# A hybrid encoder layer on one core: taps from on-chip tiles, bias halves, spreads by transposes, value products moved ahead

## The chip, the cores and the metric

The kernel runs on one core of one Trainium2 chip. The core has TensorE (PE, matrix products; its weight loads are listed apart as PEld), VectorE (DVE), ScalarE (ACT), GpSimd (POOL) and SyncE (SP, which only issues transfers here). Data lives in DRAM, in the on-chip memory of 128 partitions, and in eight banks in which TensorE leaves its sums. POOL and SP issue the transfers, each from a queue in program order. The metric is the time of one execution in microseconds on the device. Before the change the median of three runs is 2327.94 us (2321.54 to 2329.34).

## The reference

One layer of an encoder over 2048 frames of width 1024. After one RMS norm a single projection feeds two groups:

```python
h = rmsnorm(x, norm_mix_g)
proj = h @ w_in                     # u_ssm (512) | q (512) | k (512) | v (512)
y_ssm = s5_mixer(u_ssm, ...)        # 32 groups of 16 channels, 64 complex states each
y_att = chunked_attention(q, k, v, rel_bias)   # 8 heads of 64
x = x + concat(rmsnorm(y_ssm), rmsnorm(y_att)) @ w_out
h2 = rmsnorm(x, norm_ffn_g)
x = x + (silu(h2 @ w_gate) * (h2 @ w_up)) @ w_down
return rmsnorm(x, norm_final_g)
```

The state space group computes `b_bar = (exp(lam dt) - 1) / lam * b`, runs the recurrence `state = lam_bar * state + b_bar u`, and puts out `Re(C state) + D u`, then a GELU and a sigmoid gate. In attention each chunk of 64 frames sees itself and the 8 chunks before it, and every score gets a bias of its head, indexed by the distance clipped to 128:

```python
rel = arange(576)[None, :] - 512 - arange(64)[:, None]
bias = rel_bias[:, clip(rel, -128, 128) + 128]
scores = q @ k.T / 8 + bias ;  probs = softmax(scores)
```

## The kernel before

All products are float32 made of three passes over operands split into a rounded high part and a low part (`split`, `mm3`): high by high, high by low, low by high. TensorE's products go through `Ordered`, so their order is the order in which the program states them; the other engines' instructions are placed by a scheduler, with `high_priority` pulling some ahead.

`u_phase` computes the state space input. It walks four blocks of 512 frames in the order 1, 2, 3, 0. `prep(b)` loads eight tiles `xt` (a ring of four), scales and splits them, and loads the rows of `x` for the sums of squares. `group(b, f)` is one product of 128 outputs by 512 frames, 24 passes, and a block has four. `finish(b)` spreads the block's reciprocal roots over the partitions (`spread_`, which calls `spread`) and scales and stores the four results to `u`. Between the groups `long(n)` advances `n` steps of `ssm_prologue`.

`ssm_prologue` makes the constants of the state space part. Its elementwise work on VectorE gives powers `pr`, `pi` of `lam_bar` and the scaled input matrix `bbr`, `bbi`. Each tile holds two groups of a pair: partitions 0 to 63 one, 64 to 127 the other. `v` (four blocks `b_`, from `cmul`) is the output side, stored to DRAM as `vs`, and `wt` the input side. The 32 tap matrices `kt` (16 by 128 each) are products of `bb` and `v` per group. For these the kernel stores `bbr` and `bbi` to DRAM (`bbs`), reloads them and `vs` with the real and imaginary halves of one group under one another on 128 partitions (`bbg`, `vg`), and takes one product per group. `transposes` turns the `wt` tiles and stores them as `bsts`. POOL fills a table of powers `a8`. The last steps run inside the first query product, where `PRO` says how many follow each of its steps.

`att_phase` runs 128 steps (4 blocks by 8 heads by 4 query tiles). A step s takes the scores of its tile (`scores`), the transposes of step s - 2 (`transp`), the value products of a finished head (`pv_head`), once in two heads the division by the softmax sums (`pv_scale`), and then a share of the units: projections of queries, keys and values, and eight state space units (`ssm_unit`) of 15 steps, whose recurrence runs on POOL. A `Unit` counts how many of its steps are due at s; the first value projection `v0` has 17 and is due in steps 0 to 3. The scores bank is one buffer: VectorE adds the bias and takes the minimum out of it (line 829) before the next scores go in.

The bias of a head is a tile `nb` of 128 by 640. A preparation turns the table into rows `nbs` in DRAM (8 by 768), spreads them with a copy inside DRAM to `nbms`, row p shifted by p (line 521), and two more copies put 1e30 into two corners of each head (line 524), so that what lies outside the band drops out. `load_nb` (line 800) then loads one head's tile, two buffers in turn, two steps ahead.

A spread is four products of a column, repeated 128 times, with the identity: in `spread`, in `rstd_steps`, and in `pv_scale`.

After attention `mix_phase` gates, normalises and projects, and the gate, up and down products follow by a seven-product scheme; the change touches them only through the spreads.

Of the kernel before, what the change touches and what calls it, by code (L numbers as in the profile page):

```python
# [13 lines left out]
ALU = mybir.AluOpType  # L14
AX = mybir.AxisListType

P = 128
# [3 lines left out]
NG, CH, NS = 32, 16, 64  # L21
NPR = NG // 2
L = 8
# [24 lines left out]
V0 = 0, 4  # L48
DB, XB = 3, 2
# [15 lines left out]
LONG = 1, 3, 2  # L65
# [56 lines left out]
def spread(k, te, pb, o, c):  # L122

    for i in range(4):
        te.matmul(pb[:, i * P : (i + 1) * P], o[:, c + i : c + i + 1].to_broadcast([P, P]), k.ident[:], start=True, stop=True)


def rstd_steps(k, te, psum, pool, tag, sq, n, out, **kw):
# [11 lines left out]
    for i in range(nt):  # L140
        te.matmul(pb[:, i * P : (i + 1) * P], o[:, i : i + 1].to_broadcast([P, P]), k.ident[:], start=True, stop=True)
# [15 lines left out]
def ssm_prologue(k, ident, S):  # L157
# [3 lines left out]
    with tc.tile_pool(name="pro", bufs=1) as p:  # L161
# [126 lines left out]
        def transposes(b_, wt):  # L288
            bst = k.t(p, "v" if b_ > 1 else "vg", [P, 9 if b_ > 1 else 8, 2, NS], bufs=2)[:, :8]
# [42 lines left out]
        for g2 in range(2):  # L332
            for c, bt in ((0, bbr), (1, bbi)):
                nc.gpsimd.dma_start(S["bb"][:, g2, c].rearrange("q n m -> n q m"), bt[g2 * NS : (g2 + 1) * NS])
        yield
        wts = []
        for b_ in range(4):
            qs = slice(4 * b_, 4 * b_ + 4)
# [7 lines left out]
            yield  # L346
        for b_ in range(4):
            qs = slice(4 * b_, 4 * b_ + 4)
            wt = [k.t(p, f"wt{i}", [P, 4, L, CH], bufs=4) for i in range(2)]
            cmul(wt[0][:], wt[1][:], rc(pr, qs), rc(pi, qs), cc(bbr, qs, L), cc(bbi, qs, L), [4, L, CH])  # L350
            wts.append(wt)
            yield
# [13 lines left out]
        kt = k.t(p, "kt", [CH, 8, P], bufs=2)  # L366
        nc.gpsimd.memset(kt[:], 0.0)
        for b_ in range(4):
            nc.gpsimd.dma_start(S["kt"][:, 8 * b_ : 8 * b_ + 8, 0], kt[:])
        bb = k.t(p, "bbg", [P, NG, CH])  # L370
        nc.sync.dma_start(bb[:], S["bb"].rearrange("q g c n m -> (c n) (q g) m"))
        dm = k.t(p, "cm1", [P, 576])[:CH, : NG * CH].rearrange("c (g m) -> c g m", g=NG)
        V.tensor_tensor(dm, ident[:CH, :CH].unsqueeze(1).to_broadcast([CH, NG, CH]),
                        ddt[:].unsqueeze(2).to_broadcast([CH, NG, CH]), op=ALU.mult)
        vgs = []
        for b_ in range(4):
            vgs.append(k.t(p, "vg", [P, 8, P], bufs=2)[:] if b_ < 2 else k.t(p, "v", [P, 9, P], bufs=2)[:, :8])
            nc.sync.dma_start(vgs[b_], S["v"].rearrange("q g c n m -> (c n) (q g) m")[:, 8 * b_ : 8 * b_ + 8, :P])
        for b_ in range(4):
            gs = slice(8 * b_, 8 * b_ + 8)  # L380
            vg = vgs[b_]
            kt = k.t(p, "kt", [CH, 8, P], bufs=2) if b_ < 2 else k.t(p, ("bc", "small")[b_ - 2], [CH, 8, P])
            if b_ == 0:
                yield
            for g0 in (0, 4):
                ps = k.t(k.pro_psum, "pp", [P, 512])[:].rearrange("p (a b) -> p a b", a=4)
                for g in range(4):
                    k.te.matmul(ps[:CH, g, :], bb[:, 8 * b_ + g0 + g, :], vg[:, g0 + g, :], start=True, stop=True)
                nc.scalar.copy(kt[:, g0 : g0 + 4, :], ps[:CH])
                yield  # L390
            V.tensor_tensor(kt[:, :, :CH], kt[:, :, :CH], dm[:, gs], op=ALU.add)
            nc.gpsimd.dma_start(S["kt"][:, gs, 1], kt[:])
# [4 lines left out]
def u_phase(k, ident, S, aw):  # L397
# [3 lines left out]
    with ExitStack() as cx:  # L401
# [113 lines left out]
        for n in range(1, NSB):  # L515
            last, b = BLOCKS[n - 1 : n + 1]
            prep(b)
            if n == 1:
                corner = k.t(p1, "corner", [64, 64])
                nc.gpsimd.memset(corner[:], 1e30)  # L520
# [1156 lines left out]
```

## Time and profile before

| | us | where it is from |
|---|---|---|
| median of three runs | 2327.94 | times (2321.54 to 2329.34) |
| the profiled execution | 2328.99 | its own time |
| its span | 2327.2 | profile |
| TensorE busy | 2197.0 | page, part 1 |
| weight loads busy | 1852.3 | page, part 1 |
| VectorE busy | 1545.0 | page, part 1 |
| ScalarE busy | 1004.7 | page, part 1 |
| GpSimd busy | 349.0 | page, part 1 |
| mean granted clock of TensorE | 0.973 | cores view |

The busy time of an engine is the union of its instructions. Weight loads overlap products. A row of the stretch view gives, for a stretch of the span, the busy time of each engine with its count of instructions, the granted clock of TensorE (1.00 is full), the busy share of the 16 transfer engines, and GB/s. The chain of waits is followed back from the last instruction to what released it; a piece that begins with DMA is time in which the next engine waited for that transfer. A row of SP's queue shows the time taken to issue, not to land.

### The profile page before, as it was taken

What the parts mean: (1) busy time and instruction counts of PE and PEld (TensorE: products, weight loads), DVE (VectorE), ACT (ScalarE), POOL (GpSimd) and SP (SyncE); (2) the same over time, 40 slices, a digit from 0 to 9 for tenths busy, and PEclk for the clock granted to TensorE, in tenths of its full rate; (3) what the DMA queues carried; (4) which work ended last, traced back from release to release, by engine and by line L of the source; (5) the groups of instructions that cost most, each with busy time, mean ns of one, the idle gap of its engine ahead of it and who ended that gap; (6) DMA issues with size and microseconds to landing.
All of it is one profiled execution on the core that took longest, in us unless ns stands there. A gap on an engine that the chain in (4) does not pass through costs nothing.

```text
span 2327.2 us, 30433 instructions
## 1 busy us (share of the span) xinstructions
PE 2197.0 (94%) x10712; PEld 1852.3 (80%) x10712; DVE 1545.0 (66%) x2695; ACT 1004.7 (43%) x1655; POOL 349.0 (15%) x814
## 2 busy tenths in 40 slices
PE   8878899999997899999999999999999989999997
PEld 6766688898986688878888887888888878888886
DVE  7746545756545756777776668666756477789766
ACT  4435445555556752253333336333333343353321
POOL 3237545466542000000000000000000000000000
PEclk9989899999998999999999999999999999999998
DMA  8967676775654434763554647555423297465641
GB/s 274 291 221 249 194 209 196 200 221 176 193 153 146 141 105 149 245 198 127 182 180 149 235 160 284 183 198 163 167 90 114 68 338 255 163 216 186 227 158 73
DMA packets 225329, 434.90 MB, mean 187 GB/s; under 512 B 43480, under 2 KB 70152, under 8 KB 218072
## 3 DMA queue, kind: packets, MB, share of 16 engines
q1 hardware_dynamic: 220312, 418.79, 55.0%
q0 software_dynamic: 4864, 14.17, 1.9%
q8 instruction: 84, 1.38, 0.2%
q14 instruction: 69, 0.57, 0.1%
HBM read 292.88 MB, written 132.15 MB: 183 GB/s over the span
## 4 chain that ended last, share of the span: by engine, by line
PE 82%; DMA 6%; DVE 6%; POOL 2%; ACT 2%; issue 1%; SPq 1%; DVEq 0%; ACTq 0%; POOLq 0%
PE X L78 20%; PE ps L78 19%; PE Y L78 10%; PE pf L78 10%; PE big L78 9%; PE W L78 5%; PE pj L78 5%; PE sc L78 2%; PE pt L81 2%; DMA xt<-in_xp 2%; DMA xt<-in_xt 1%; DVE lo L154 1%; SPq L549 1%; DMA nb<-nbms 1%; DMA hd<-wc 0%
## 5 line engine op out<-in xcount | busy, mean ns | idle before, releaser
L78 PE MATMUL X<-hi,c 128*128 128x512 f32 x1408 | 451.3, 391 | 8.5 <-DVE c L154 6.9
L78 PE MATMUL ps<-hd,hd 128*128 128x512 f32 (+1 forms) x1968 | 432.0, 382 | 6.1 <-ACT hd L154 3.7
L78 PEld LDWEIGHTS ps<-hd,hd 128*128 128x128 f32 x1968 | 359.3, 190 | 77.5 <-ACT hd L154 4.6
L78 PEld LDWEIGHTS X<-hi,c 128*128 128x128 f32 x1408 | 265.6, 189 | 65.2 <-DVE c L154 7.8
L78 PE MATMUL X<-lo,c 128*128 128x512 f32 x704 | 274.9, 390 | 0.0
L154 ACT CAST hd<-hd 128x1536 fp32r<-128x1536 f32 (+1 forms) x106 | 147.6, 1393 | 238.1 <-DMA hd<-hq 181.9
L78 PE MATMUL Y<-hi,c 128*128 128x512 f32 x704 | 224.1, 389 | 1.5 <-DVE u L1367 1.5
L154 DVE TENSOR_TENSOR hd<-hd 128x1536 fp32r<-128x1536 f32 (+1 forms) x106 | 174.1, 1645 | 28.8 <-ACT hd L154 28.1
L154 DVE TENSOR_TENSOR c<-S,c 128x512 fp32r<-128x512 f32 x176 | 120.9, 688 | 104.1 <-ACT c L154 104.1
L829 DVE CUSTOM_DVE_ANT_0 s<-sc,nb 128x640 f32<-128x640 f32 (+4 forms) x128 | 94.5, 738 | 110.9 <-PE sc L78 98.7
L1491 DVE TENSOR_TENSOR acc<-acc,ps 128x512 f32<-128x512 f32 x196 | 131.3, 684 | 53.0 <-PE ps L78 48.3
L1363 ACT COPY u<-X 128x512 f32<-128x512 f32 x132 | 77.6, 588 | 204.9 <-PE X L78 204.8
L78 PE MATMUL big<-m,woh 128*128 128x512 f32 x512 | 162.7, 400 | 0.0
L78 PE MATMUL pf<-hi,w 128*128 128x512 f32 x416 | 153.1, 420 | 8.9 <-ACT w L154 4.6
L154 ACT CAST c<-S 128x512 fp32r<-128x512 f32 x176 | 109.5, 622 | 118.3 <-PE Y L78 67.0
L78 PEld LDWEIGHTS Y<-hi,c 128*128 128x128 f32 x704 | 132.1, 188 | 29.3 <-DVE u L1367 1.9
L78 PEld LDWEIGHTS X<-lo,c 128*128 128x128 f32 x704 | 132.8, 189 | 27.7
L154 ACT CAST c<-raw 128x512 fp32r<-128x512 f32 x132 | 82.2, 623 | 149.4 <-PE Y L78 71.2
L78 PE MATMUL Y<-lo,c 128*128 128x512 f32 x352 | 137.0, 389 | 0.0
L832 ACT ACTIVATE s<-s,mn 128x640 f32<-128x640 f32 (+4 forms) x128 | 98.0, 765 | 77.2 <-DVE mn L829 76.5
L848 DVE TENSOR_TENSOR ptl<-pt,pth 128x640 fp32r<-128x640 f32 (+3 forms) x152 | 98.3, 647 | 45.8 <-ACT pth L847 44.1
L847 ACT CAST pth<-pt 128x640 fp32r<-128x640 f32 (+3 forms) x152 | 83.7, 551 | 94.8 <-PE pt L81 89.5
(441 smaller groups left out, 4229.3 us busy)
## 6 DMA issues: line engine op xcount, KB each, us to landing
w<-wss SPq DMA_DIRECT2D x36, 1024.0 KB, 6.7
hq<-g SPq DMA_DIRECT2D x140, 256.0 KB, 2.2
hd<-hq SPq DMA_DIRECT2D x42, 768.0 KB, 4.4
hd<-wc SPq DMA_DIRECT2D x42, 768.0 KB, 6.0
raw<-in_w_gate SPq DMA_DIRECT2D x44, 512.0 KB, 3.7
raw<-in_w_up SPq DMA_DIRECT2D x44, 512.0 KB, 4.1
wc<-px SPq DMA_DIRECT2D x66, 256.0 KB, 3.2
wss<-w SPq DMA_DIRECT2D x12, 1024.0 KB, 6.0
```

The lines of the kernel that those rows point to most:

```text
L78: return self.tc.keep_in_program_order(self.tc.nc.tensor.matmul(*a, **b))
L81: return self.tc.keep_in_program_order(self.tc.nc.tensor.transpose(*a, **b))
L154: return nc.scalar.copy(hi, raw), nc.vector.tensor_tensor(lo, raw, f32(hi), op=ALU.subtract)
L549: ins = nc.sync.dma_start(out, in_)
L829: nc.vector.tensor_tensor_reduce(s[:, :nk].rearrange("p (a b) -> p a b", a=nch), ps[:, :nch, :half], hd.nb[:, nk - 1 :: -1].rearrange("p ( ...
L832: nc.scalar.activation(s[:, :nk], s[:, :nk], AF.Exp, bias=mn[:], scale=-1.0, accum_out=sums[sb, pr][:, hh, qp : qp + 1])
L847: nc.scalar.copy(pth[:, a:b, qp, :], pt[:, a:b, :])
L848: nc.vector.tensor_tensor(ptl[:, a:b, qp, :], pt[:, a:b, :], f32(pth[:, a:b, qp, :]), op=ALU.subtract)
L1363: nc.scalar.copy(u[:], ps[:])
L1491: V.tensor_tensor(a, a, ps[:], op=ALU.add)
```

## The change

Five parts:

- The taps are products of the on-chip tiles: for each pair, the real and the imaginary part of `bbr`/`bbi` and `v` add up over two passes, separately for partitions 0 to 63 and 64 to 127, into two banks. The store `bbs` and the loads `bbg`, `vg` and `v` go. A list `LONGS` gives the order of output tiles (`VO`), input tiles (`WI`) and taps (`TA`), one entry for each `long` step, and `u_phase` calls `long(1)` between groups.
- `nbms` and its copies go. Two tiles hold the bias for heads in turn: `nba`, allocated ahead of all and loaded for head 0 during block 2, and `nbb`. Their corners are set once on chip; a head's load is two transfers of 64 partitions by 576, straight from `nbs`.
- The spreads use the transpose of TensorE in place of a product.
- `v0` is advanced by 8 steps (`VFIRST`), two of its four tiles, ahead of the first score.
- The turning of `wt` is spread over four steps of the first query product, where it followed the taps before.

```diff
+VFIRST = 8
-LONG = 1, 3, 2
+VO, WI, TA = range(3)
+LONGS = ((VO, 0),), ((VO, 1),), ((TA, 0), (VO, 2)), ((TA, 1), (VO, 3)), ((TA, 2), (WI, 0)), ((TA, 3), (WI, 1)), ((WI, 2),), ((WI, 3),)
...
-        te.matmul(pb[:, i * P : (i + 1) * P], o[:, c + i : c + i + 1].to_broadcast([P, P]), k.ident[:], start=True, stop=True)
+        te.transpose(pb[:, i * P : (i + 1) * P], o[:, c + i : c + i + 1].to_broadcast([P, P]), k.ident[:])
...
+        def taps(b_):
+            kt = k.t(p, "kt", [CH, 8, P], bufs=2)
+            gs = slice(8 * b_, 8 * b_ + 8)
+            pss = [k.t(k.pro_psum, "pp", [P, 512])[:].rearrange("p (a b) -> p a b", a=4) for _ in range(2)]
+            for q in range(4):
+                for c, bt in enumerate((bbr, bbi)):
+                    for g2, ps in enumerate(pss):
+                        rows = slice(g2 * NS, (g2 + 1) * NS)
+                        k.te.matmul(ps[:CH, q, :], bt[rows, 4 * b_ + q, :], vts[b_][c][rows, q, :L, :].rearrange("p k c -> p (k c)"), start=c == 0, stop=c == 1)
+            for g2, ps in enumerate(pss):
+                nc.scalar.copy(kt[:, g2::2, :], ps[:CH])
+            V.tensor_tensor(kt[:, :, :CH], kt[:, :, :CH], dm[:, gs], op=ALU.add)
+            nc.gpsimd.dma_start(S["kt"][:, gs, 1], kt[:])
...
-        bb = k.t(p, "bbg", [P, NG, CH])
-        nc.sync.dma_start(bb[:], S["bb"].rearrange("q g c n m -> (c n) (q g) m"))
...
-            nc.sync.dma_start(vgs[b_], S["v"].rearrange("q g c n m -> (c n) (q g) m")[:, 8 * b_ : 8 * b_ + 8, :P])
...
-                    k.te.matmul(ps[:CH, g, :], bb[:, 8 * b_ + g0 + g, :], vg[:, g0 + g, :], start=True, stop=True)
...
-                nc.sync.dma_start(S["nbm"][:], bass.AP(S["nb"].tensor, S["nb"].offset + 1, [[768, H], [1, P], [1, 640]]))
...
+                bias_corners(k, S["nba"])
+                bias_rows(k, S, 0, S["nba"])
...
-            long(LONG[n - 1])
+            long(1)
...
-            now += [group(b, f, f in pf) for f in (1, 2)]
+            for f in (1, 2):
+                now.append(group(b, f, f in pf))
+                if n > 1:
+                    long(1)
...
+def bias_corners(k, nb):
+    for m in range(2):
+        k.nc.gpsimd.memset(nb[m * 64 : m * 64 + 64, m * 576 : m * 576 + 64], 1e30)
+
+def bias_rows(k, S, h, nb):
+    src = bass.AP(S["nb"].tensor, S["nb"].offset + h * 768 + 65, [[1, 64], [1, 576]])
+    k.nc.sync.dma_start(nb[:64, 64:], src)
+    k.nc.sync.dma_start(nb[64:, :576], src)
+    return nb
...
-            nb = k.t(aa, "nb", [P, 640], bufs=2)
-            nc.sync.dma_start(nb[:], S["nbm"][h])
-            return nb
+            return bias_rows(k, S, h, nbt[h % 2])
...
-                k.ta.matmul(pb[:, i * P : (i + 1) * P], rb[:, i].rearrange("p h d -> p (h d)"), ident[:], start=True, stop=True)
+                k.ta.transpose(pb[:, i * P : (i + 1) * P], rb[:, i].rearrange("p h d -> p (h d)"), ident[:])
...
+        nbt = S["nba"], k.t(aa, "nbb", [P, 640])
+        bias_corners(k, nbt[1])
...
+        for _ in range(VFIRST):
+            next(v0)
...
-            units.append(Unit(v_unit(sb, 0), V_N, g0 + C[1], g0 + C[2], 2, light=LIGHT) if sb else Unit(v0, V_N, *V0, done=1))
+            units.append(Unit(v_unit(sb, 0), V_N, g0 + C[1], g0 + C[2], 2, light=LIGHT) if sb else Unit(v0, V_N, *V0, done=1 + VFIRST))
```

More of the change, by code (lines that the diff above doesn't have):

```diff
@@ L140, in rstd_steps @@
     for i in range(nt):
[L141 removed]
+        te.transpose(pb[:, i * P : (i + 1) * P], o[:, i : i + 1].to_broadcast([P, P]), k.ident[:])
     k.nc.scalar.copy(out, pb[:, : nt * P])
@@ L351, in ssm_prologue @@
             wts.append(wt)
+        for make in LONGS:
+            for m, b_ in make:
+                (outputs, inputs, taps)[m](b_)
             yield
@@ L364, in ssm_prologue @@
             G.tensor_copy(S["sw"][:, n, 1, :], a8[:, 1, :, e])
[L366 to L369, printed above, removed]
-        bb = k.t(p, "bbg", [P, NG, CH])
-        nc.sync.dma_start(bb[:], S["bb"].rearrange("q g c n m -> (c n) (q g) m"))
[L372 to L377, printed above, removed]
-            nc.sync.dma_start(vgs[b_], S["v"].rearrange("q g c n m -> (c n) (q g) m")[:, 8 * b_ : 8 * b_ + 8, :P])
[L379 to L387, printed above, removed]
-                    k.te.matmul(ps[:CH, g, :], bb[:, 8 * b_ + g0 + g, :], vg[:, g0 + g, :], start=True, stop=True)
[L389 to L392, printed above, removed]
+        yield
         for b_ in range(4):
```

34 lines of the change are left out of this document (16 added, 18 removed).

## Prediction

> **What bounds the kernel now.** I read the page first, then the busy time by stretches, then the chain that ended last, and inside its two gaps the DMA issues and single instructions.
>
> ```profile
> PE 2197.0 (94%) x10712; PEld 1852.3 (80%) x10712; DVE 1545.0 (66%) x2695; ACT 1004.7 (43%) x1655; POOL 349.0 (15%) x814
> ```
>
> TensorE is busy 94% of the span, so only its own work or its gaps matter. The stretches show where the gaps lie (columns: stretch, length, busy time of each engine, granted clock, DMA share, GB/s).
>
> ```profile
> 60.00:76.00 16.00, 9.65 (x26) 6.29 (x27) 5.74 (x8) 7.61 (x11) 0.00 (x0) 0.79 0.74 253
> 76.00:136.00 60.00, 60.00 (x307) 48.71 (x306) 49.96 (x98) 23.84 (x39) 24.70 (x57) 1.00 0.88 286
> 136.00:160.00 24.00, 7.85 (x59) 6.34 (x57) 6.77 (x11) 8.88 (x23) 9.45 (x18) 0.82 0.92 293
> 160.00:180.00 20.00, 19.87 (x117) 18.48 (x118) 6.51 (x18) 7.29 (x20) 0.00 (x0) 0.87 0.21 49
> 180.00:340.00 160.00, 133.38 (x720) 113.02 (x719) 91.14 (x198) 82.58 (x204) 91.07 (x194) 0.91 0.74 227
> 340.00:765.00 425.00, 397.15 (x2446) 359.22 (x2444) 243.37 (x436) 239.47 (x454) 205.89 (x511) 0.97 0.61 180
> ```
>
> Two stretches are bad: 60 to 76 us and 136 to 160 us, both on ground that the change touches. Between them TensorE has no gap. The chain names the causes (start, length, what).
>
> ```profile
> 34.68 28.46 DMA xt<-in_xp x2
> ...
> 66.69 7.00 DMA xt<-in_xp
> ...
> 76.01 0.89 PE pp L78 x8
> ...
> 99.58 16.36 PE ps L78 x72
> ...
> 120.95 1.85 PE pp L78 x16
> ...
> 133.10 2.28 PE pf L78 x9
> 135.40 0.75 DVE xt L740 x2
> ...
> 138.88 4.32 DMA lo0x<-lo0x
> 143.57 2.66 PE pf L78 x22
> 146.23 13.31 DMA nb<-nbms
> 160.13 0.76 PE sc L78 x2
> 160.90 4.79 PE pf L78 x24
> 165.69 0.36 PE sc L78 x2
> ...
> 180.00 1.73 PE pj L78 x8
> ```
>
> Gap one: the third block's `xt` tiles arrive late. Gap two: VectorE cannot take the first score before the first bias tile `nb` has landed, 13.31 us after its issue.
>
> ```profile
> 36.48 0.80 SPq L521 DMA_DIRECT2D nbms<-nbs  x1
> 37.61 15.93 SPq L440 DMA_DIRECT2D xt<-in_xp  x4
> ```
>
> Why `xt` is late: right ahead of those loads on SP's queue stands the copy that spreads the bias into DRAM, and the four loads behind it take 15.93 us only to be issued.
>
> ```profile
> nb<-nbms SPq DMA_DIRECT2D x32, 320.0 KB, 4.6
> nbms<-nbs SPq DMA_DIRECT2D x1, 2560.0 KB
> vg<-vs SPq DMA_DIRECT2D x2, 512.0 KB, 7.1
> v<-vs SPq DMA_DIRECT2D x2, 512.0 KB, 4.9
> ```
>
> **The change, part by part.**
>
> *Bias without the DRAM copy.* The 2560 KB `nbms` copy goes; it is read and written, so 5.2 MB at the 253 to 286 GB/s of the stretches is 10 us of DMA if both sides run at once and 20 us if they add. In its place `nba` gets two loads of 64x576 (288 KB together). In 60 to 76 us TensorE did 26 matmuls; by the 72 that took 16.36 us a 512-column pass is 0.227 us, so 26 are 5.9 us and 10.1 us were lost to waiting and to the slow clock (0.79). Bounds: 3 us come back if the 4-deep `xt` ring, which VectorE frees only after its scale work, is late next; 11.5 if not even the issue delays ahead of 60 us stay. I take 10: the freed DMA time alone covers it.
>
> *Spreads as transposes.* One spread is four 128x128 products that run as eight passes (`pp` x8, 0.89 us: 0.111 a pass). What a transpose runs as is seen on the tiles that are transposed already:
>
> ```profile
> L81 PE MATMUL pt<-ident,s 128*128 128x128 f32 x560 | 84.9, 278 | 10.7 <-DVE ptl L848 10.7
> L78 PE MATMUL pj<-ident,rb 128*128 128x128 f32 x128 | 17.0, 276 | 0.1
> L78 PE MATMUL big<-ident,no 128*128 128x128 f32 x80 | 11.0, 291 | 7.8 <-DVE no L112 7.8
> L78 PE MATMUL ps<-ident,no 128*128 128x128 f32 x32 | 4.8, 298 | 4.3 <-DVE no L112 4.3
> L78 PE MATMUL pp<-ident,no 128*128 128x128 f32 x32 | 4.4, 282 | 0.0
> ```
>
> The program has 560 such transposes and the trace 560, while the 64 products of `rb` show as 128: half the passes. A spread falls from 8 x 0.111 to 4 x 0.111, by 0.44 us. There are 16 in attention (128 passes), 4 in the prologue, and with two small ones outside these rows 16 later. Four save 1.8 us ahead of 120 us; the other 32 could save 14.1 us, of which I take 11, because next to some of them TensorE waits for VectorE anyway (bounds 5 and 14).
>
> *Taps from on-chip tiles.* The DRAM copy `bb`, its load and the four loads `vg`/`v` (2 MB) go. TensorE reads the halves in place: 64 products over 64 partitions instead of 32 over 128, so 128 passes instead of 64. Before, 16 passes are 1.85 us, 7.4 in all; 128 at that rate are 14.8, so +7.4. Their place moves from inside the first query product to the ends of block products, where 76 to 136 us has no idle time: all of it is on the path. They also wait for VectorE's `v` tiles, and two of those tiles are then written again behind the taps; VectorE has 10 us to spare in that stretch, so I cost these waits at nothing, and up to 3 us if that cover goes. Bounds of the taps: 0 if two halves run side by side, and +27.5 if every pass stood alone at the row's latency:
>
> ```profile
> L78 PE MATMUL pp<-vg,bbg 128*16 128x128 f32 x32 | 3.8, 273 | 0.0
> ```
>
> (128 x 0.273 = 34.9, less 7.4.) I take +7.4, the rate of the nearest row. The Trainium skill, "TensorE: Matmul & The Clock Gate", Part 3 on packing small matmuls, says that products in different row groups run concurrently; by that the two halves, which alternate in the new order, would cost 0 extra. The Trainium skill's page "TensorEngine Tiling (Array Packing)", Key Properties, speaks against the change: switching the tiling mode drains TensorE, and the four tap groups switch it eight times. No row here has 64-row products, so neither is shown.
>
> *Transposes of the input weights* (32 passes, 3.5 us) now stand wholly inside the first query product; before, 20 of them came after it.
>
> *Half of the first value products ahead of the first score.* 48 of 96 products move in front of score 0; before, 22 of them ran between score 0 and score 1. From the end of the query product to score 0 runs a chain over VectorE, ScalarE and a DMA that the change leaves alone: 135.40 to 143.2, 7.8 us. The 48 products fit under it at the full rate, which a later row gives as 0.120 each:
>
> ```profile
> 454.51 2.87 PE pf L78 x24
> ```
>
> 48 x 0.120 = 5.8, less the wait for their second weight split. So 26 products (3.1 us) leave the stretch behind it at no cost. The price: score 1 follows score 0 with nothing between, and each waits until VectorE has read the one bank pair: about 0.5 us for scores 1, 2 and 3, 1.5 in all.
>
> *More bias loads per head.* SP issues two loads of 64 rows in place of one, 32 more issues. Slack of a head's bias, by one head in mid-attention:
>
> ```profile
> 602.87 0.32 SPq L800 DMA_DIRECT2D nb<-nbms  x1
> ...
> 610.18 0.81 DVE L829 CUSTOM_DVE_ANT_0 s<-sc,nb 128x640 f32<-128x640 f32 x1
> ```
>
> 7.3 us from issue to use, against the 4.6 of the landing: nothing as long as the second half lands by then. A second issue of 0.3 us is covered by the same slack. The first `nbb` load now waits for two stores of transposed weights from POOL's queue, and with it the state space loads queued behind it on SP, which before began here:
>
> ```profile
> 149.73 10.97 SPq L549 DMA_DIRECT2D U<-u  x8
> ```
>
> I allow 1 us for that (0 to 4).
>
> **The sum.** End of the first query product: 135.4 - 10.1 - 1.8 + 7.4 + 3.5 = 134.4. Score 0 at 134.4 + 7.8 = 142.2, score 1 at 143.1 instead of 160.13: 17.0 us earlier. To the 3.1 for the moved products comes the slow clock after the gap: 24 products in 4.79 instead of 2.87 us, and 0.76 instead of 0.36 in score 1, so 2.3. Less 1.5 and 1: at the first state product (180.00) the kernel is 17.0 + 3.1 + 2.3 - 2.5 = 19.9 us ahead. From 180 to 340 us TensorE idles 26.6 us on transfers and on POOL; these hang on the steps, not on the clock, but I let 2 us be lost there. 19.9 - 2 + 11 = 29 us. The profiled execution took 2328.99 us (span 2327.2 and 1.8 around it), 1.05 above the median of 2327.94; 2329 - 29 = 2300, and I give 2300 for the median. The forecast's own range is 2292 to 2310. About 0.3% (7 us) is what a measurement of this kernel tells from no change.
>
> **Rivals.**
> - *Halves of the taps run side by side.* Then the 7.4 us are not paid: 2293. For it: the halves alternate and write different banks. Against: every row here is over 128 partitions. The Trainium skill's Part 3 rule is this case.
> - *The third block is late anyway.* If the `xt` ring or ScalarE's squares hold back the loads, gap one stays for the most part and the gain is 8 us less: 2308. For it: the loads go in four at a time. Against: 15.93 us of issue right behind the one large copy.
> - *A new wait takes the place of the bias wait.* The state space loads were issued only from 149.73 us on; if they land no earlier than before, the first state product stalls until about 170 and half of the 19.9 is lost: 2310. For it: POOL's stores stand ahead of them, and those follow POOL's power table. Against: 160 to 180 us shows a DMA share of 0.21, so before they were long there.
> - *Slower: the bias halves land late in every head.* All 64 rows of a load read the same 3 KB of DRAM. With 31 heads and 7.3 us of slack the gain is gone from a landing of 7.3 + 29/31 = 8.2 us on; at 9.5 us it would be 31 x 2.2 = 68 us, so 2368. For it: the first bias load took 13.31 us. Against: that was at a DMA share of 0.92, and the old copy read just so: 2560 KB are 8.9 times these 288, done when the `xt` behind it landed, 26.7 us after its issue (34.68 + 28.46 - 36.48), 3.0 us each.
> - *The copy did nothing to gap one and the bias wait is another engine's:* no change, 2328. Against: both rows above.
>
> **Chances.** Forecast 0.48, side by side 0.20, block late 0.13, new wait 0.12, slower 0.05, no change 0.02. Faster: 0.48 + 0.20 + 0.13 + 0.12, less 0.01 for several small losses together: 0.92; same 0.02, slower 0.06. The range goes from 2282 (side by side 7.4, all spreads on the path 3, nothing lost later 3, gap one at its bound 1.5: 2285, and 3 for the runs' own spread) to 2320 (a new wait at 2310, spreads at 5 instead of 11, VectorE's cover gone 3: 2319); slower and no change, 0.08, lie outside it.
>
> **What would show it.** 60 to 76 us without idle and with the clock near 1; VectorE reading score 0 as soon as it is there, with no wait for `nb`; spread passes halved in count; the tap products at about 0.115 us each, or in pairs. Wrong would be: idle before the first state product, VectorE waiting for `nba` or `nbb` in the heads, taps far above 15 us.

## The result, and the profile after

The changed kernel takes 2301.06 us (median of four runs, 2299.45 to 2301.38) against 2327.17 us for the kernel before, measured beside it (2321.54 to 2329.34): a ratio of 0.989, 95% interval 0.9872 to 0.9908. That is 26 us less; 2300 was forecast. The profiled execution took 2301.02 us with a span of 2299.2. The total is right, but several of its terms are not, and they offset one another, so that it comes out within about 1 us is in part luck. The engines' row on the page:

```profile
PE 2179.8 (95%) x10632; PEld 1835.0 (80%) x10632; DVE 1546.0 (67%) x2695; ACT 1001.9 (44%) x1655; POOL 344.9 (15%) x813
```

The 80 matmuls fewer are those that the change asks for: 144 less for 36 spreads, 64 more for the taps.

The busy time by stretches of the changed kernel (columns as in the prediction: stretch, length, busy time and count of each engine, granted clock, DMA share, GB/s):

```profile
60.00:76.00 16.00, 15.29 (x90) 11.76 (x91) 12.96 (x30) 12.21 (x21) 3.49 (x6) 1.00 0.87 306
76.00:136.00 60.00, 56.28 (x355) 46.23 (x354) 42.93 (x72) 17.76 (x35) 29.40 (x68) 0.99 0.66 222
135.00:140.00 5.00, 0.79 (x2) 0.50 (x2) 2.46 (x6) 1.33 (x4) 1.25 (x7) 0.51 1.02 333
136.00:160.00 24.00, 20.55 (x110) 18.43 (x111) 10.23 (x26) 10.31 (x28) 0.42 (x4) 0.81 0.60 174
180.00:340.00 160.00, 133.00 (x719) 113.26 (x719) 89.68 (x189) 79.11 (x188) 86.90 (x214) 0.90 0.72 208
```

Gap one is gone: 60 to 76 us now holds 90 matmuls at full clock, where it held 26 at 0.79. Gap two has shrunk but not gone: in 135 to 140 us TensorE works 0.79 us of five, with the transfer engines full (1.02). The chain of waits (start, length, what) and the waits from 100 to 160 us (who waits for what: us in all, times, longest) say why:

```profile
131.09 4.96 DMA bsts<-bc
136.15 0.48 ACT v L799
138.19 0.48 DVE v L800
138.93 0.81 PE sc L80 x2
157.03 1.73 PE pj L80 x8
204.37 6.94 DMA XG<-X
```

```profile
DVE v L800 <- ACT v L799: 10.1, 2, 5.6
ACT v L799 <- DMA bsts<-bc: 5.8, 1, 5.8
PE sc L80 <- DVE mn L842: 5.6, 2, 5.0
```

The chain from the first query product to score 0, from the time lines of VectorE and TensorE: the product is scaled, TensorE runs the last pass of score 0, VectorE reads it (start, length, operation, idle before and its end):

```profile
125.71 1.37 DVE L755 TENSOR_TENSOR xt<-pf,rsn 128x512 f32<-128x512 f32 x2 [5.56 <-PE pf L80]
...
133.56 0.33 PE L80 MATMUL sc<-hi2x,lo0x 128*128 128x128 f32 x1 [0.76 <-DMA lo0x<-lo0x]
...
138.58 0.28 DVE L842 CUSTOM_DVE_ANT_0 s<-sc,nba 128x128 f32<-128x128 f32 x1
```

Hardly anybody waits for a bias tile any more (one wait of 0.4 us in the whole run). Instead ScalarE waits 5.8 us, before it writes the first value tile `v`, for a store of transposed weights: `v` is placed on the memory of `bc`, the tile that `transposes` had filled and was still sending to `bsts`. VectorE's part of `v` (L800) stands in its queue ahead of the first score, so score 0, whose last pass starts on TensorE at 133.56 us, is read only at 138.58 us. It was the value products, moved ahead of score 0, that brought this wait there.

The lead of the changed kernel, from the same matmul or the same reading of a score in the two traces:

| work | before, at | after, at | lead, us |
|---|---|---|---|
| second block's second product | 42.9 | 38.9 | 3.9 |
| third block's first product, first pass | 63.9 | 55.4 | 8.5 |
| third block's first product, late part | 79.3 | 64.6 | 14.65 |
| behind the first group of taps | 82.4 | 70.6 | 11.8 |
| behind the second | 88.8 | 79.7 | 9.1 |
| behind the third | 99.9 | 93.2 | 6.7 |
| behind the fourth | 106.3 | 101.7 | 4.6 |
| VectorE scales the first query product | 135.4 | 125.7 | 9.7 |
| score 1 is read | 161.0 | 139.8 | 21.3 |
| first state product | 179.8 | 156.9 | 23.0 |
| score 36 is read | 334.1 | 317.8 | 16.3 |
| score 126 is read | 750.2 | 733.7 | 16.4 |
| end of the span | 2327.2 | 2299.2 | 28.0 |

So 23 us are won by the first state product, 7 are lost up to score 36, attention adds nothing, and 11 to 12 more come behind it.

### The profile page after: what moved, and what is told of

It is laid out like the page before. It is cut to its first block, busy times and chain, and to the rows that moved or that the text cites. A ratio compares the mean times of both kernels' runs of the same rounds, so it can differ in the third digit from the quotient of the medians.

```text
span 2299.2 us, 30276 instructions
## 1 busy us (share of the span) xinstructions
PE 2179.8 (95%) x10632; PEld 1835.0 (80%) x10632; DVE 1546.0 (67%) x2695; ACT 1001.9 (44%) x1655; POOL 344.9 (15%) x813
## 4 chain that ended last, share of the span: by engine, by line
PE 79%; DVE 6%; DMA 4%; POOL 2%; issue 2%; ACT 2%; SPq 1%; DVEq 0%; ACTq 0%; POOLq 0%
PE X L80 20%; PE ps L80 19%; PE Y L80 10%; PE big L80 9%; PE pf L80 8%; PE W L80 5%; PE pj L80 4%; PE sc L80 2%; PE pt L83 2%; DMA xt<-in_xt 1%; SPq L564 1%; DVE lo L156 1%; DMA hd<-wc 0%; DMA Tm<-kts 0%; DMA ya_s<-ya 0%
## 5 line engine op out<-in xcount | busy, mean ns | idle before, releaser
L1384 DVE TENSOR_TENSOR u<-u,Y 128x512 f32<-128x512 f32 x88 | 60.4, 687 | 83.1 <-ACT u L1380 60.8
```

The source lines that it names most:

```text
L1384: V.tensor_tensor(u[:], u[:], ps[:], op=ALU.add)
```

## Experiments

Each kernel was timed beside the kernel before. Ratios are to the runs of the kernel before that stand beside it. Leads are of the profiled execution over that of the kernel before, at the reading of a score by VectorE.

| kernel | median, us | ratio, 95% interval | lead at score 1 | 16 | 36 | 126 | profiled execution, us |
|---|---|---|---|---|---|---|---|
| changed | 2301.06 | 0.989, 0.9872 to 0.9908 | 21.3 | 21.9 | 16.3 | 16.4 | 2301.02 |
| before_with_bias_halves | 2320.06 | 0.9963, 0.995 to 0.9977 | 21.6 | 22.6 | 13.1 | 14.0 | 2319.34 |
| before_with_transposes | 2318.04 | 0.9952, 0.9936 to 0.9968 | 2.5 | 1.0 | -0.9 | 2.2 | 2315.56 |
| bias_copy_added | 2305.54 | 0.99, 0.9881 to 0.9918 | 14.6 | 14.4 | 16.6 | 17.3 | 2300.05 |
| taps_one_half_at_a_time | 2303.19 | 0.9891, 0.9873 to 0.9908 | 16.3 | 17.6 | 16.0 | 19.3 | 2304.23 |
| spreads_back | 2323.6 | 0.9975, 0.9961 to 0.9989 | 16.8 | 17.0 | 10.6 | 8.2 | 2324.91 |
| mix_spreads_back | 2318.21 | 0.9951, 0.9933 to 0.9969 | 21.0 | 21.8 | 19.6 | 19.5 | 2315.2 |
| attention_spreads_back | 2308.47 | 0.9918, 0.9904 to 0.9932 | 19.6 | 19.1 | 17.8 | 16.0 | 2302.55 |
| no_value_first | 2305.2 | 0.9892, 0.9874 to 0.991 | 18.4 | 16.7 | 17.1 | 15.2 | 2308.31 |
| stores_out_of_the_way | 2290.8 | 0.9833, 0.9817 to 0.9849 | 23.8 | 26.6 | 28.6 | 28.6 | 2291.75 |
| stores_out_no_value_first | 2298.2 | 0.9871, 0.9853 to 0.989 | 17.5 | 16.0 | 18.6 | 21.5 | 2295.93 |
| stores_out_whole_value_first | 2295.84 | 0.986, 0.9843 to 0.9877 | 20.3 | 26.8 | 30.1 | 31.6 | 2290.9 |
| second_half_from_pool | 2352.97 | 1.0098, 1.0079 to 1.0117 | 24.8 | 18.0 | 16.9 | -29.0 | 2353.12 |

Executions of one of these kernels lie up to 15 us apart (mix_spreads_back: 2309.11 to 2323.61), so the places in the traces say more than the medians where less than 5 us is asked. But each trace is one execution, and its places scatter too: at the second block's second product the versions of the changed kernel lead by 1.5 to 4.1 us, and from score 126 to the end the lead grows by 4.9 to 11.6 us in the ten kernels whose spreads there are transposes, while it shrinks by 4.1 to 5.7 in the three that have products there, as the kernel before has. What makes these differences was not traced.

### The bias part alone, the transposes alone

The first is the kernel before with the change's hunks for `nba`, `nbb`, `bias_corners` and `bias_rows` and nothing else; the second has only its three hunks on the spreads. Their cores:

```diff
-                nc.sync.dma_start(S["nbm"][:], bass.AP(S["nb"].tensor, S["nb"].offset + 1, [[768, H], [1, P], [1, 640]]))
+                bias_corners(k, S["nba"])
+                bias_rows(k, S, 0, S["nba"])
...
-            nc.sync.dma_start(nb[:], S["nbm"][h])
-            return nb
+            return bias_rows(k, S, h, nbt[h % 2])
```

```diff
-        te.matmul(pb[:, i * P : (i + 1) * P], o[:, c + i : c + i + 1].to_broadcast([P, P]), k.ident[:], start=True, stop=True)
+        te.transpose(pb[:, i * P : (i + 1) * P], o[:, c + i : c + i + 1].to_broadcast([P, P]), k.ident[:])
```

> The kernel before with the bias part of the change alone: no copy of the bias inside DRAM, two tiles with their corners set on chip, two loads of 64 partitions for each head. Prediction: gap one gives back 10.1 us, and VectorE no longer waits for the first bias tile, so score 1 comes 17 to 23 us earlier than 160.1 us and the first state product 17 to 20 us earlier than 180.0; no head waits for its bias. What of this reaches the end: by the sum nearly all, 2328 - 18 = 2310; by the runs so far, in which a lead of 6 us ahead of score 0 was gone at score 36, a third is lost and it is 2314 to 2318. Rival, the old taps, which wait for loads from DRAM inside the first query product, take the place of the bias wait: first state product less than 10 us earlier, 2320 or more.

> The kernel before with the spreads as transposes and nothing else. Prediction: 12.8 us less, 2315. By the runs so far: 20 spreads on the path (4 ahead of score 0, 16 behind attention) by 0.44 are 8.8 us, those of attention are nothing, so 2319; and whatever order VectorE's instructions take at the passage from mix to gate products, where the kernel before waits 4.8 us, the changed one 2.1 and the one with products in the mix phase alone 8.4: 2316 to 2323 with it. Rival, the gain of the spreads in the changed kernel hangs on its other parts: under 4 us, 2324 or more.

The bias part alone leads by 21.6 us at score 1 and 23.8 at the first state product (155.9 us), as much as the whole change; the old taps do not take its place. But 9.5 of 22.6 us are gone at score 36, more than the third that I allowed, and 2320 comes out of it, above the 2314 to 2318 expected (the time of the rival, without its mechanism). Behind score 126 another 4.4 us of the lead go (14.0 there, 9.6 at the end of the span), where this part changes nothing: 1.8 of them fit the passage from the mix to the gate products, at which TensorE waits 6.6 us here and 4.8 in the kernel before; the rest is open. The transposes alone give 2318, between the 2315 of the prediction and the 2319 of the runs: 2.5 us at score 1, none by score 120 (0.5), and the rest behind attention. The two parts make 9 and 11 us by their medians, 20 of the 26. The taps, the moved value products and the turned weights were not run apart from them in this way; together they account for about 5 us, or the parts do not add.

### Copy put back

```diff
+                nc.sync.dma_start(S["nbm"][:], bass.AP(S["nb"].tensor, S["nb"].offset + 1, [[768, H], [1, P], [1, 640]]))
                 bias_corners(k, S["nba"])
```

> The changed kernel with the old 2560 KB copy of the bias inside DRAM put back at its old place on the queue of SP, ahead of the loads of the third block; nothing reads it, and the two copies into its corners stay out. Theory of the prediction, the copy alone makes gap one: the stretch of 60 to 76 us shows again about 10 us of TensorE idle, the third block begins 10 to 14 us later than in the changed kernel, and the end is at about 2301 + 10 = 2311. Rival, the third block is late for other reasons and the gap closed because the taps and the bias loads moved: less than 3 us at the third block, 2301 to 2304. A middle way: the block is late by 10 us, but the tap groups and the value products behind it have slack on VectorE and DMA, and only some 5 us reach the end: 2306.

SP's queue in the changed kernel, and with the copy in it (start, time to issue, line, transfer):

```profile
33.55 0.53 SPq L552 DMA_DIRECT2D nba<-nbs  x1
34.12 0.79 SPq L553 DMA_DIRECT2D nba<-nbs  x1
35.01 3.57 SPq L444 DMA_DIRECT2D xt<-in_xp  x4
```

```profile
33.70 0.77 SPq L523 DMA_DIRECT2D nbms<-nbs  x1
34.52 5.98 SPq L553 DMA_DIRECT2D nba<-nbs  x1
40.54 4.02 SPq L554 DMA_DIRECT2D nba<-nbs  x1
44.66 5.03 SPq L444 DMA_DIRECT2D xt<-in_xp  x4
```

The landing of the first bias tile, in the list of DMA issues from 30 to 70 us, in the same order (last column, median us to landing):

```profile
nba<-nbs SPq DMA_DIRECT2D x2, 144.0 KB, 9.1
```

```profile
nba<-nbs SPq DMA_DIRECT2D x2, 144.0 KB, 24.4
```

The issue of each load behind the copy stretches from 0.5 or 0.8 us to 4 to 6, the `xt` loads start 9.65 us later, and the third block's products are 7 to 8 us behind the changed kernel. So the copy makes 8 of the 14.65 us of lead at the third block, somewhat less than the 10 to 14 expected: TensorE waits 4.4 us for that block's first split tile. This idle time lies ahead of 60.5 us, and not in 60 to 76 us as expected; there the clock is 0.82. The first state product comes 6.4 us later. But nothing of it can be seen at the end: at score 36 this kernel is level with the changed one, and the ratios (0.99, 0.989) cannot be told apart. The gain in gap one and what reaches the end are two things.

### Taps one half at a time

```diff
-            for q in range(4):
-                for c, bt in enumerate((bbr, bbi)):
-                    for g2, ps in enumerate(pss):
+            for g2, ps in enumerate(pss):
+                for q in range(4):
+                    for c, bt in enumerate((bbr, bbi)):
```

> The changed kernel with the order of the tap products turned: all eight products of partitions 0 to 63 first, then all eight of partitions 64 to 127, instead of the two halves in turn. The trace of the changed kernel shows a group of 32 tap passes in 1.85 us, as long as 16 passes over 128 partitions took before. Theory, halves run side by side when they alternate: without a neighbour of the other half each group takes 3.7 us, the four groups cost 7.4 more (the term of the prediction), score 0 comes about 7 us later than in the changed kernel, and the end is at 2306 to 2308. Rival, a pass over 64 partitions is simply half as long: the order is nothing, a group stays at 1.85 us and the time at 2301.

TensorE's time line in the second tap group, first of the changed kernel, then of this one (start, length, then the count of passes in the row):

```profile
76.80 0.40 PE L80 MATMUL pp<-v,bbi 64*16 64x128 f32 x4 [0.33 <-DVE v L288]
77.03 0.39 PE L80 MATMUL pp<-v,bbr 64*16 64x128 f32 x4
77.25 0.39 PE L80 MATMUL pp<-v,bbi 64*16 64x128 f32 x4
```

```profile
78.54 0.39 PE L80 MATMUL pp<-v,bbi 64*16 64x128 f32 x2 [0.39 <-DVE v L288]
78.77 0.38 PE L80 MATMUL pp<-v,bbr 64*16 64x128 f32 x2
78.99 0.38 PE L80 MATMUL pp<-v,bbi 64*16 64x128 f32 x2
```

A row comes every 0.22 us in both; with the halves in turn it holds four passes, otherwise two. Two passes over different halves of the partitions run side by side, and the order decides it: 0.055 us a pass against 0.11. (The Trainium skill, "TensorE: Matmul & The Clock Gate", Part 3: Packing small matmuls, says that products in distinct row groups run concurrently; these rows agree.) Score 0 comes 5 us later, short of 7, in part because in the other order no group waits for ScalarE's `pb` (0.8 us in the changed kernel); the end does not change (0.9891). The theory holds for the passes and fails for the end.

### Spreads back

Products again in all three places, or only behind attention (`norm` with its own four products, and `rstd_steps`; the two other `spread` calls there stay transposes, so that 14 of the 16 are back), or only in attention (`pv_scale`, the last pair of lines):

```diff
-        te.transpose(pb[:, i * P : (i + 1) * P], o[:, i : i + 1].to_broadcast([P, P]), k.ident[:])
+        te.matmul(pb[:, i * P : (i + 1) * P], o[:, i : i + 1].to_broadcast([P, P]), k.ident[:], start=True, stop=True)
...
-                k.ta.transpose(pb[:, i * P : (i + 1) * P], rb[:, i].rearrange("p h d -> p (h d)"), ident[:])
+                k.ta.matmul(pb[:, i * P : (i + 1) * P], rb[:, i].rearrange("p h d -> p (h d)"), ident[:], start=True, stop=True)
```

> The changed kernel with all spreads as products again (four 128x128 products each, in all three places). Forecast of the prediction: 1.8 us are lost ahead of 120 us and 11 after it, so 2301 + 12.8 = 2314, spread over attention and the mix phase alike (16 spreads each, about 5.5 and 5.5). Rival, from the trace of the changed kernel, whose lead over the kernel before stayed at 16.4 to 15.1 us from score 43 to score 120: the 16 spreads of attention lie beside other waits and cost nothing either way; only the 16 others and the 4 of the prologue count, 20 x 0.44 = 8.8, so 2310, and score 120 comes at most 2.5 us later than in the changed kernel.

> The changed kernel with only the 16 spreads behind attention (norms of the mix phase, and the roots of the last norms) as products again; the 4 of the prologue and the 16 of attention stay transposes. All spreads back cost 22.5 us, of which 5 to 8 us were lost by score 127 and some 16 behind it, while 16 spreads by 0.44 us are 7. Theory, all these spreads lie on TensorE's path, and the rest is order: VectorE's and ScalarE's instructions at the passage from mix to gate products were placed in another order. Then each pair of spreads moves the end by 0.9 us (7 us in all), nothing changes ahead of score 120, and the passage (5 us there) decides between 2308 (same passage as in the changed kernel) and 2314 (the slower one comes back). Rival, a spread as a product costs a whole us on the path: 2317 with losses of 1 us at each spread. Rival, what is lost behind attention comes from the state at its end: under 2305.

> The changed kernel with only the 16 spreads of attention (division by the softmax sums) as products again. Prediction: these are part of the 11 us, so about 5.5 us, spread evenly over the stretch from score 8 to score 127: 2306.5. Rival, from the two traces: they lie beside waits of TensorE in steps that other engines pace; score 120 comes less than 2 us later, and the end is at 2301 to 2303.

All back costs 22 us by the medians, 20 by the ratios, against the forecast's 12.8. The 16 of attention cost nothing that the trace shows: score 120 is read 0.1 us earlier than in the changed kernel, and the profiled execution took 2302.55. Its five executions reach up to 2312.61, though, and the median is 7 us above the changed kernel; I leave this open. The 14 behind attention cost 14 to 17 us. From 744 to 982 us of the changed kernel the loss of spreads_back grows by 5.3 us, in steps of 0.9 at each pair of spreads, just 0.44 to 0.46 for each. The rest is not the spreads themselves. TensorE's waits from 960 to 1030 us in the changed kernel and with the mix spreads back:

```profile
PE X L80 <- DVE c L156: 2.1, 1, 2.1
```

```profile
PE X L80 <- ACT c L156: 5.8, 1, 5.8
PE X L80 <- DVE c L156: 2.6, 1, 2.6
```

VectorE's queue there, in the same order (start, length, operation; L1362 and L1363 are one statement):

```profile
985.02 1.22 DVE L1106 TENSOR_TENSOR xt<-xt,big 128x1024 f32<-128x1024 f32 x1 [1.79 <-PE big L80]
986.16 0.69 DVE L1362 TENSOR_TENSOR S<-raw 128x512 f32<-128x512 f32 x1
986.76 0.69 DVE L156 TENSOR_TENSOR c<-raw,c 128x512 fp32r<-128x512 f32 x1
```

```profile
988.61 2.46 DVE L1107 TENSOR_TENSOR xt<-xt,big 128x1024 f32<-128x1024 f32 x2 [4.21 <-DMA xt<-in_xt]
994.40 0.69 DVE L1114 TENSOR_TENSOR sa<-sa,xt 128x512 f32<-128x512 f32 x1 [3.33 <-ACT xt L1113]
995.01 0.69 DVE L1363 TENSOR_TENSOR S<-raw 128x512 f32<-128x512 f32 x1
```

With products in the mix phase, the scheduler puts the sum of squares `sa`, which waits 3.33 us for ScalarE, ahead of the operands `S` and `c` of the first gate product. TensorE loses 8.4 us at this passage in place of 2.1; the kernel before, with yet another order, loses 4.8 (3.4 and 1.4). So the theory of mix_spreads_back holds, with its slower passage (2315.2 in the profiled execution, 2314 expected): 14 spreads by 0.44 are 6 us of direct cost, this passage is another 6 by its order, and the remaining 2 to 5 us are not assigned.

### The stores out of the way of the value tiles

```diff
-            bst = (k.t(p, "v", [P, 9, 2, NS], bufs=2) if b_ < 2 else k.t(p, ("bc", "small")[b_ - 2], [P, 8, 2, NS]))[:, :8]
+            bst = (k.t(p, "v", [P, 9, 2, NS], bufs=2) if b_ < 2 else k.t(p, "kt", [P, 8, 2, NS], bufs=2))[:, :8]
```

Instructions and their order stay the same on TensorE, VectorE, ScalarE and SP; only the place of two tiles differs.

> The changed kernel with the third and fourth of the transposed weight tiles (bst) in the memory of the tap tiles kt instead of the tiles bc and small. In the changed kernel the first value tile v lies on the memory of bc and so waits 5.8 us for a store of it; VectorE, which reads the scores, stands behind that v tile in its queue. Theory, that store is the wait that took the place of the bias wait: score 0 is read at about 134 us instead of 138.58, score 1 at about 135.3 instead of 139.76, the loads of the first state space unit are issued 4 us earlier, the first state product moves from 157.0 to about 152.5, and the end from 2301 to 2296 or 2298 (a third of such a lead was lost between 180 and 300 us). Rival, the transfer engines are full from 130 to 145 us and the next wait (second weight split, the copies of q, U and Tm) comes just as late: first state product earlier by less than 1.5 us, 2300 to 2301.

The wait for `bsts` is gone: VectorE reads score 0 0.36 us after the start of its last pass, where it took 5.0 in the changed kernel (TensorE, then VectorE):

```profile
135.98 0.33 PE L80 MATMUL sc<-hi2x,lo0x 128*128 128x128 f32 x1 [0.76 <-DMA lo0x<-lo0x]
136.34 0.29 DVE L842 CUSTOM_DVE_ANT_0 s<-sc,nba 128x128 f32<-128x128 f32 x1 [0.15 <-PE sc L80]
```

Score 0 is read at 136.3 us all the same, and not at the 134 expected, since in this execution the first query product is scaled 2.4 us later (128.15 against 125.71 us); and the loads `U` of the state space unit are issued no earlier (138.9 us in both). The stretches of this kernel read:

```profile
135.00:140.00 5.00, 3.32 (x24) 2.79 (x23) 2.12 (x9) 2.55 (x8) 3.97 (x15) 1.00 0.99 316
136.00:160.00 24.00, 22.93 (x133) 19.91 (x134) 9.77 (x28) 12.59 (x35) 6.57 (x19) 1.00 0.90 266
```

The first state product comes at 152.1 us, 4.7 earlier, as expected. The end gains 10 us by the medians, 13 by the ratios, twice as much: 2290.8 (2288.48 to 2292.14), and its interval (0.9817 to 0.9849) lies clear of the changed kernel's. This version beats both kernels. Of the added gain, 4.2 us come between scores 16 and 17, where TensorE waits for `XG`, the rearranged states. The stretch from score 16 to score 17 in the changed kernel and in this one:

```profile
203.76:217.76 14.00, 9.32 (x41) 7.85 (x42) 4.75 (x11) 3.91 (x10) 1.52 (x3) 0.76 0.64 167
```

```profile
199.00:208.80 9.80, 6.63 (x41) 5.93 (x42) 4.75 (x10) 3.91 (x10) 1.52 (x3) 1.00 0.74 224
```

and TensorE's wait in it, in the same order:

```profile
PE pj L80 <- DMA XG<-X: 4.5, 1, 4.5
```

```profile
PE pj L80 <- DMA XG<-X: 2.9, 1, 2.9
```

The same 41 matmuls take 9.32 us behind a stall of 4.5 us, and 6.63 behind one of 2.9: 1.6 us more of waiting cost 2.7 more by the clock (0.76 against 1.00). (The Trainium skill, "TensorE: Matmul & The Clock Gate", Part 1: The HAM clock gate, has the clock fall to half after an idle window of about 3.4 us; these two stalls lie on either side of it, others of the changed kernel do not.) There a stall of 3.00 us is followed by half the clock, and one of 3.26 us is not, so the length of a stall alone does not decide it. The first matmul behind each and the stretch that follows:

```profile
309.18 1.62 PE L80 MATMUL pj<-U,Bst 128*128 128x256 f32 x3 [3.00 <-DMA Tm<-kts]
309.20:312.50 3.30, 3.30 (x9) 2.67 (x9) 0.00 (x0) 1.20 (x4) 0.00 (x0) 0.50 0.45 110
```

```profile
191.09 0.52 PE L83 MATMUL pt<-ident,s 128*128 128x128 f32 x3 [3.26 <-DVE ptl L861]
191.10:194.60 3.50, 3.48 (x23) 3.05 (x24) 1.97 (x6) 1.33 (x4) 2.95 (x9) 1.00 1.02 429
```

### How much of the value projection to move

0 in the changed kernel, then 0 and 16 in the kernel with the stores out of the way:

```diff
-VFIRST = 8
+VFIRST = 0
```

> The changed kernel with no value product ahead of score 0 but the usual first step (VFIRST = 0); nothing else changes. By the prediction the move took 3.1 us of products off the path and cost 1.5 for the scores, so it undoes a gain of 1.6 us and the clock's share: first state product 2 to 4 us later, 2303 to 2305. Rival, in this kernel the move itself brought the wait of the value tile for the store bsts in front of score 0: without it score 0 is read at 134 us, score 1 comes at about 135, and the 48 products that are now behind cost 5.8 us and the wait 3 to 4: the first state product moves by -1 to +3, the time stays within 2299 to 2304.

> The kernel with the stores out of the way, and no value product ahead of score 0. There the move is priced without the wait for bsts: theory, 26 to 48 products fill the 8 us before score 0 in which TensorE else waits for the copies of q: without them the first state product comes 4 to 6 us later than in that kernel (152.1) and the time goes from 2290.8 to about 2295. Rival, the time of that kernel comes from what happens behind the first state product (waits for the gathers XG and the clock behind them), and the move is worth less than 2 us: 2289 to 2293.

> The kernel with the stores out of the way, and all 96 products of the first value projection ahead of score 0 (VFIRST = 16). Theory: the time in front of score 0 that waits for the copies of q is filled by the first 48 already (TensorE idles 1.7 us of 132 to 140 us there); 48 more put score 0 off by 4 to 5 us, and scores 1 to 3 then follow one another with nothing between, 1 to 2 us: first state product 0 to 2 us later than 152.1, 2290 to 2294. Rival, the loads of the first state space unit and the bias halves have then more time before they are needed, and the stall at step 16 goes: up to 3 us faster, 2288.

In the changed kernel the move is worth nothing that can be measured (0.9892 against 0.989): it brings 2.8 us at the first state product, together with its own wait, and loses them at score 17. With the stores out of the way it is worth 7 us (0.9871 against 0.9833, intervals apart). Moving all of it puts score 0 off by 3.5 us and leads again by 1.4 at the first state product; the profiled execution is 0.9 us faster than with half, the median 5 us slower, and the intervals overlap. No gain is shown.

### Second half of the bias from POOL's queue

```diff
-    k.nc.sync.dma_start(nb[64:, :576], src)
+    k.nc.gpsimd.dma_start(nb[64:, :576], src)
```

> The kernel with the stores out of the way, and the second half of each head's bias (partitions 64 to 127) loaded from POOL's queue instead of SP's; the first half stays on SP. It asks where a third of the lead goes between score 16 and score 36: in the kernels with two bias loads on SP, the loads of xt and of the weights w for the next block stand later in SP's queue (the third of the eight xt loads behind the loads of the state space unit, not ahead of them; the second half of a bias and a w load behind xt loads that wait for their buffer), and scores 24 to 29 take 30.1 us instead of 27.0 before, 32.8 with the bias part alone. Theory, this order costs 3 to 5 us: with one load on SP, whose queue then has the order of the kernel before there, scores 24 to 29 take 27 to 28 us and the end is at 2286 to 2288. Rival, the lead is lost because the same bytes have to move in less time, whatever their order: 30 us again, 2290 to 2292. Rival, POOL issues the half late, behind its scans, and each issue costs 0.6 us there: VectorE waits for nba and nbb in the heads, 2293 or more.

The last rival came nearest, but the loss is far larger, 2353, slower than the kernel before, and most of it comes another way. The waits from 140 to 760 us:

```profile
POOL nba L553 <- DVE mn L842: 66.7, 5, 20.2
POOL nbb L553 <- DVE mn L842: 60.9, 3, 21.6
DVE s L842 <- DMA nbb<-nbs: 12.8, 2, 9.9
DVE s L842 <- DMA nba<-nbs: 11.0, 2, 6.0
```

POOL cannot issue the load before VectorE has read the old tile for the last time, up to 21.6 us, and the recurrence of the state space units stands behind it in POOL's queue. VectorE's 23.8 us of waiting for late halves are the smaller part. From score 24 to score 27 no lead is lost (24.0 and 24.2), which the theory on SP's order would give, but behind that the other effect covers all; the question of the run stays open.

## Why the prediction was right, point by point

- **Gap one, -10.1: right.** With the bias part alone the late part of the third block's first product comes 10.0 us earlier, and the copy put back costs 7 to 8 there. The full change has 14.65 at this place, above the bound of 11.5, but 3.9 of it were won in the second block, where the kernel before waits for split tiles and its clock is 0.89 from 40 to 50 us (1.00 after). The bias part alone has 0.4 there, so this comes from another part, about 0.5 of it from the spread; the rest I did not separate.
- **Taps, +7.4: mis-sized.** The four groups took 2.8, 2.7, 2.4 and 2.1 us off the lead, 10.1 in all, against 14.8 charged, and the old 7.4 go: net +2.7. The rival that the halves run side by side was true: 128 passes by 0.055 are 7.0 us; my nearest row was one of 128 partitions, and its rate did not carry over. The rest are waits and switches between passes over 128 and over 64 partitions, at which a pass starts 0.32 us after the one before in place of 0.23 (75.62 and 75.94 us): about 0.1 us for each of eight. The side-by-side rival's 2293 did not follow, since what is won ahead of score 0 is mostly not kept.
- **Cover of VectorE for the taps at nothing: nearly right.** One of the four groups waits for VectorE's `v` (`[0.33 <-DVE v L288]` in the row above), the fourth for nothing; two wait 0.4 us each for ScalarE, which copies the spread out (`pb`), and that wait the sum does not have.
- **End of the first query product, 134.4.** It came earlier: VectorE scales it at 125.7, not at 134.4, since the gap and the taps were both better than charged.
- **7.8 us from there to score 0, "left alone": right up to TensorE, wrong for the reading.** From the scaled query product to the last pass of score 0 the chain took 7.85 us (125.71 to 133.56; before, 135.40 to 143.24), but VectorE read it 5.0 us later, 12.9 in all. I asked who waits for the moved products' results on TensorE, and not what their evacuation waits for: memory in which a store was still under way. With the stores elsewhere the 5.0 are 0.36. This is the rival of a new wait in the bias wait's place, at another spot than I put it (I named the state space loads). The errors in these two steps, 8.7 early and 5.1 late, mostly cancel, which is luck: score 1 is 3.3 us ahead of the forecast 143.1.
- **19.9 us at the first state product:** 23.0. From score 1 on the lead grows by 1.7 us, against the 2.9 of the sum (3.1 + 2.3 - 2.5).
- **2 us lost from 180 to 340: wrong.** 7 were lost by score 36 in the full change, 9.5 with the bias alone. "These hang on the steps, not on the clock" did not hold: scores 24 to 29 took 27.0 us before and 30.3 after, by longer waits for the split tiles of the next block (`hi` and `lo`, 4.9 us before, 8.2 after), and the stall at score 16 cost the clock as well. With the stores out of the way scores 24 to 29 take as long, 30.1, and yet the lead at score 36 is larger than at score 16. The kernel before with transposes alone needs 29.9 us for them, too, with 7.7 us of waits for `hi` and `lo`, though it has a lead of only 0.7 us at score 24 and the bias loads of the kernel before. So these 3 us need neither an early lead nor a second bias load on SP's queue, and a part of what I call lost is not lost by the lead. Why one early lead is kept and another is not stays open.
- **Spreads, 11 us behind 120 us.** 11 to 12 came, all behind attention: about 7 by the passes of 16 spreads, 2.7 by the passage to the gate products (4.8 us of waiting before, 2.1 after), a matter of order. With transposes alone the passage is at 2.1 too. The other 2 lie within the scatter behind score 126 named above, and so may part of the agreement. The 16 of attention gave nothing at the profiled places (lead 16.3 at score 36, 15.1 at score 120), where I had counted half of the term.
- **Bias per head at nothing: right.** But for one wait of 0.4 us for `nba` no head waits; the transfers land in 4.8 us in the median, 7.5 at the most, against 7.3 of slack, as the answer on tile `nbb` has it (`nba`: 4.1 and 9.3):

```profile
DMA to landing us min/median/max: 2.8/4.8/7.5
```

The rival on the other side (late halves) did not occur, but second_half_from_pool shows its mechanism, and that it is worse through what queues behind the load than through the load.

## What to carry to other kernels

Work that is moved ahead of a wait needs a place for its results, too: ask what still reads or sends from that memory, and give a store that ends late a tile that nobody needs soon. A lead won early is not a gain until the stages behind it have been passed; here differences of 5 to 7 us at score 0 (the copy, the order of the taps) were gone at score 36, and one of 5 at the first state product doubled, so measure at several places and not at the end alone. And when one operation becomes shorter, a scheduler may order others anew: compare the order on each engine before crediting the operation with the difference.

## What the runs showed of the hardware that I had not expected

Products over 64 partitions that alternate between the two halves run in pairs: a row of four passes each 0.22 us, against two in the other order. A stall of 4.5 us lowered the clock of what follows (0.76, 41 matmuls in 9.32 us), one of 2.9 us did not (1.00, 6.63 us); but one of 3.00 us did (0.50 behind it), and one of 3.26 us did not (1.00). Two small loads queued right behind a 2560 KB copy inside DRAM took 5.98 and 4.02 us only to be issued, and 24.4 us in the median to land, against 0.53, 0.79 and 9.1 us without the copy.
